# Residual products 512 columns wide by token tile, with weights kept whole, norms a tile behind, and the FFN in three parts

## The chip, the cores and the metric

The kernel runs on one core of one Trainium2 chip. The metric is the device time of one execution in microseconds (us); lower is better, and the median of several executions counts. TensorE (PE) does matrix products and transposes, VectorE (DVE) and ScalarE (ACT) work element by element, GpSimd (POOL) does a few tiny operations, and SyncE (SP) issues nearly all loads.

## The reference

Two layers over two streams of 256 tokens each: the latents (stream 0) and a context (stream 1), with 1024 features. The context is needed in layer 0 alone; layer 1 computes the latents only. Cut to what matters here:

```python
hx = modulate(rmsnorm(x, mix_pre_g[l]), shx1, scx1)          # and hc for the context
yx, yc = mixer_layer(hx, hc, ...)    # four branches, gates, their sum @ w_out
x = x + gx1 * rmsnorm(yx, mix_post_g[l])
fx = swiglu(modulate(rmsnorm(x, ffn_pre_g[l]), shx2, scx2), w_ffn1[l], w_ffn3[l], w_ffn2[l])
x = x + gx2 * rmsnorm(fx, ffn_post_g[l])
# shifts, scales and gates of a layer: silu(c) @ ada_w[l] + ada_b[l], six rows of 1024
def swiglu(h, w1, w3, w2):           # d_ff = 2816, 22 tiles of 128
    return (jax.nn.silu(h @ w1) * (h @ w3)) @ w2
```

## The kernel before

All values are float32. A product is made of three passes over parts in the type float32r: each operand is split into a high part h (one copy on ScalarE, L87) and a low part l (one subtraction on VectorE, L90), and `gemm` runs h·h, h·l and l·h (L162 to L164) for each tile of 128 along the sum. For the weights the parts are `wh` and `wl`, pairs of 128x512.

Weights are not kept on the chip. `wload` brings 512 KB at a time into one of four buffers `raw` (issued by SyncE, L126), splits it into two pairs, and calls `tick`. Each tick lets a share of background work run: the modulation vectors of a later stage, from `ada_w`. A load of 512 KB goes to a buffer `araw` (L346), which is one of the same four, and VectorE adds its columns to accumulators `acc` (L98), later turned by a STREAM_TRANSPOSE (L324) and a reduction (L325). The rate per weight pair is a constant for each stage.

The program runs, for each layer, a mixer, the product with `w_out` and a feed-forward part (FFN). By the trace: start up to 55 us, mixer 0 to 444, out 0 to about 500, FFN 0 to about 885, mixer 1 to 1134, out 1 to 1170, FFN 1 to the end. Each engine executes its instructions in a fixed order that the build decides, and it may place an instruction ahead of one that the code writes first. Pools of buffers are opened for a stage and closed after it; the memory of a stage's pool is that of the stage before it.

A residual product (`mixer` after the branches, with mT as the turned input, and the second half of `ffn`, with G) gives y, token-major, for each tile of 128 tokens: four tiles in layer 0, two in layer 1. It goes through four column blocks of 256. In each, all token tiles run together with the sum outermost, so the weights are taken as they come; ScalarE squares the result with a sum (`sq`), VectorE multiplies it by the gate row (`y`). The last block goes one token tile after the other (`last_gemm`), and each tile is normed at once: `postnorm` sums the squares (`vp`, L437), takes a reciprocal root on GpSimd (`rp`), adds to the residual stream `x`, squares that on ScalarE; `normed` takes another root (`vn`, `rn`) and scales into `y`; `turn_in` transposes it on TensorE (L171) in 8 blocks of 128, and `modulated` (after the stream's second tile) applies shift and scale (`hm`) and splits into the next stage's input h. In the FFN, G is made and used in two halves of 11 feature tiles. A residual product of the second half adds to the first half's y.

At the end of a mixer the last gate products are followed on VectorE by `th`, `m` and the split of mT (L98), and the gate rows G are made by eight L389 products.

## Time and profile before

| what | value |
| --- | --- |
| median of 3 executions | 1365.78 us (1362.2 to 1367.07) |
| span of the profiled execution | 1368.4 us |
| TensorE busy | 1309.4 us |
| VectorE busy | 998.5 us |
| ScalarE busy | 687.9 us |

The span is from the first to the last instruction of one profiled execution; no other time is listed for it. Busy times of engines overlap. TensorE's busy time includes the modelled ends of products that run into one another, so what a product costs in a row of like ones is seen from the distance of their starts.

### The profile page before, as it was taken

What the parts mean: (1) busy time and instruction counts of PE and PEld (TensorE: products, weight loads), DVE (VectorE), ACT (ScalarE), POOL (GpSimd) and SP (SyncE); (2) the same over time, 40 slices, a digit from 0 to 9 for tenths busy, and PEclk for the clock granted to TensorE, in tenths of its full rate; (3) what the DMA queues carried; (4) which work ended last, traced back from release to release, by engine and by line L of the source; (5) the groups of instructions that cost most, each with busy time, mean ns of one, the idle gap of its engine ahead of it and who ended that gap; (6) DMA issues with size and microseconds to landing.
All of it is one profiled execution on the core that took longest, in us unless ns stands there. A gap on an engine that the chain in (4) does not pass through costs nothing.

```text
span 1368.4 us, 22990 instructions
## 1 busy us (share of the span) xinstructions
PE 1309.4 (96%) x8525; PEld 1155.2 (84%) x8525; DVE 998.5 (73%) x2162; ACT 687.9 (50%) x1611; POOL 45.2 (3%) x66
## 2 busy tenths in 40 slices
PE   5998999999999989999999999888899998899997
PEld 1697777887778988889988889878799998899997
DVE  4846688777899989987457664656887887665665
ACT  2634556546555545333353333554766666555653
POOL 1021000000000010000000000100000000000000
PEclk9999999999999999999999999999999999899999
DMA  8615222223236635665556653144342435455552
GB/s 299 206 49 153 85 70 78 76 84 103 85 102 198 203 121 162 206 200 186 179 162 215 185 167 96 47 154 154 93 124 58 152 117 167 133 181 185 180 174 98
DMA packets 167940, 194.66 MB, mean 142 GB/s; under 512 B 6682, under 2 KB 141140, under 8 KB 167572
## 3 DMA queue, kind: packets, MB, share of 16 engines
q1 hardware_dynamic: 166500, 188.73, 43.7%
q0 software_dynamic: 1312, 4.46, 1.1%
q8 instruction: 67, 1.10, 0.3%
q14 instruction: 45, 0.37, 0.1%
q10 hardware_dynamic: 16, 0.00, 0.0%
HBM read 192.12 MB, written 1.05 MB: 141 GB/s over the span
## 4 chain that ended last, share of the span: by engine, by line
PE 80%; DVE 9%; DMA 4%; ACT 3%; POOL 2%; issue 2%; SPq 0%; DVEq 0%; POOLq 0%; ACTq 0%
PE g L162 23%; PE g L164 23%; PE g L163 23%; PE a L573 3%; PE a L171 3%; PE a L624 2%; DVE grp L90 1%; DVE wl L90 1%; ACT grp L87 1%; PE g L293 1%; DVE acc L98 1%; DMA ada<-in_ada_w_dram 1%; POOL rq L114 1%; DMA raw<-in_w_in_dram 1%; DVE zq L90 1%
## 5 line engine op out<-in xcount | busy, mean ns | idle before, releaser
L87 ACT ACTIVATE wh<-raw 128x512 fp32r<-128x512 f32 (+2 forms) x520 | 317.8, 620 | 354.5 <-PE g L163 136.0
L90 DVE TENSOR_TENSOR wl<-raw,wh 128x512 fp32r<-128x512 f32 (+2 forms) x520 | 346.4, 677 | 162.9 <-ACT wh L87 157.2
L162 PE MATMUL g<-h,wh 128*128 128x256 f32 (+1 forms) x1248 | 415.5, 336 | 3.6 <-DVE grp L90 1.2
L164 PE MATMUL g<-h,wl 128*128 128x256 f32 (+1 forms) x1248 | 415.2, 334 | 0.9 <-DVE wl L90 0.9
L163 PE MATMUL g<-h,wh 128*128 128x256 f32 (+1 forms) x1248 | 415.1, 334 | 0.0
L162 PEld LDWEIGHTS g<-h,wh 128*128 128x128 f32 x1248 | 235.6, 190 | 28.1 <-ACT h L87 1.8
L164 PEld LDWEIGHTS g<-h,wl 128*128 128x128 f32 x1248 | 236.7, 190 | 23.6 <-DVE wl L90 1.1
L163 PEld LDWEIGHTS g<-h,wh 128*128 128x128 f32 x1248 | 236.8, 190 | 21.7 <-DVE h L90 0.4
L98 DVE SCALAR_TENSOR_TENSOR acc<-araw,cs,acc 128x512 f32<-128x512 f32 x224 | 162.4, 749 | 78.8 <-DMA araw<-in_ada_w_dram 60.8
L164 PE MATMUL g<-wh,g 128*128 128x256 f32 x528 | 149.4, 283 | 0.0
L162 PE MATMUL g<-wh,g 128*128 128x256 f32 x528 | 149.2, 283 | 0.0
L163 PE MATMUL g<-wl,g 128*128 128x256 f32 x528 | 148.3, 281 | 0.0
L162 PE MATMUL g<-wh,h 128*128 128x256 f32 (+2 forms) x336 | 99.4, 297 | 2.2 <-DVE m L98 1.2
L163 PE MATMUL g<-wl,h 128*128 128x256 f32 (+2 forms) x336 | 99.1, 296 | 1.3 <-DVE wl L90 1.0
L163 PEld LDWEIGHTS g<-wl,g 128*128 128x128 f32 x528 | 100.0, 189 | 0.1
L162 PEld LDWEIGHTS g<-wh,g 128*128 128x128 f32 x528 | 99.4, 188 | 0.1
L164 PEld LDWEIGHTS g<-wh,g 128*128 128x128 f32 x528 | 98.9, 187 | 0.0
L164 PE MATMUL g<-wh,h 128*128 128x256 f32 (+2 forms) x336 | 98.3, 294 | 0.0
L98 DVE SCALAR_TENSOR_TENSOR th<-th,g 128x512 f32<-128x512 f32 (+1 forms) x136 | 71.3, 549 | 6.4 <-PE g L164 3.6
L162 PEld LDWEIGHTS g<-wh,h 128*128 128x128 f32 x336 | 64.2, 191 | 4.8 <-issue 1.7
L87 ACT ACTIVATE th<-g 128x512 f32<-128x512 f32 (+1 forms) x108 | 51.5, 486 | 31.3 <-PE g L164 30.3
L163 PEld LDWEIGHTS g<-wl,h 128*128 128x128 f32 x336 | 64.0, 191 | 3.4 <-DVE wl L90 2.4
(184 smaller groups left out, 1908.3 us busy)
## 6 DMA issues: line engine op xcount, KB each, us to landing
raw<-in_w_ffn_dram SPq DMA_DIRECT2D x120, 512.0 KB
raw<-in_w_in_dram SPq DMA_DIRECT2D x84, 512.0 KB
araw<-in_ada_w_dram SPq DMA_DIRECT2D x80, 512.0 KB
ada<-in_ada_w_dram SPq DMA_DIRECT2D x16, 512.0 KB
raw<-in_w_branch_dram SPq DMA_DIRECT2D x32, 256.0 KB
raw<-in_w_out_dram SPq DMA_DIRECT2D x16, 512.0 KB
raw<-in_w_ffn_dram SPq DMA_DIRECT2D x16, 384.0 KB
raw<-in_w_in_dram SPq DMA_DIRECT2D x8, 416.0 KB
```

What stands on the lines that cost most here:

```text
L87: return self.nc.scalar.activation(out, in_, func, **k)
L90: return self.nc.vector.tensor_tensor(out=out, in0=a, in1=b, op=op)
L98: return self.nc.vector.scalar_tensor_tensor(out=out, in0=a, scalar=s, in1=b, op0=op0, op1=op1)
L114: self.nc.gpsimd.tensor_tensor(out=r, in0=v, in1=self.mhalf[:, 0:n], op=ALU.pow)
L162: mm(ps, ah, bh, start=k == 0 and opens, stop=False, skip_group_check=True)
L163: mm(ps, ah, bl, start=False, stop=False, skip_group_check=True)
L164: mm(ps, al, bh, start=False, stop=last, skip_group_check=True)
L171: self.nc.tensor.transpose(out, in_, self.ident[0:k, 0:k])
L293: self.nc.tensor.matmul(ps[j][0:2], self.cs[:, :, k], raw[j, h, k], start=k == cut[j], stop=k == NK - 1)
L573: nc.tensor.matmul(ps[:, 0:nk], x, y, start=i == 0, stop=i == len(mms) - 1 and not masked)
L624: nc.tensor.matmul(po[:, 0:256], grp[:, 4, kts[k] * 128:kts[k] * 128 + 128], pt[j][:, k], start=j == 0 and k == 0, stop=j == 1 and k == n - 1)
```

## The change

`residual()` takes the place of the column blocks and of `last_gemm`. The products of a token tile are 512 columns wide, two column blocks to a tile, and go one tile after the other. So all weights of both blocks must be there for a tile to be done; for `w_out` they lie in 16 pairs of their own (tags `oh`, `ol`) in the stage's pool, for the last FFN part half of them lie in buffers of G (tag `G2`). After a tile's products comes `chain` (the norms); `turn` (transposes, shift and scale) of a tile is written behind the next tile's products, and the last tile's turn is put off: `flush` calls it in the FFN behind the first products of stream 0 (layer 0), at its beginning (layer 1), and in mixer 1 behind the first products of its branch A, which are moved ahead of the pooling branch for that. The last tile's normed result goes to a buffer of the tag `raw`. The turned features go to one fixed set of tiles, `H`, which also serves as mT. The FFN is done in three parts of 8, 8 and 6 feature tiles. The pairs wh, wl have 8 buffers each in place of 7.

```diff
-WB = 7
+WB = 8
...
+PARTS = ((0, 8), (8, 8), (16, 6))
...
+        self.late = self.qp = None
+        self.H = [tuple(self.hp.tile([128, 512], R, tag=f"h{k}{x}", name="h") for x in "hl") for k in range(NK)]
...
+    def bank(self):
+
+        self.turn8 = (self.turn8 + 1) % 8
+        return self.pg() if self.turn8 < 4 else self.pa()
...
-    def h_tiles(self, name):
-        return [tuple(self.hp.tile([128, 512], R, tag="h", name=name, bufs=16) for _ in range(2)) for _ in range(NK)]
+    def flush(self):
+
+        late, self.late = self.late, None
+        if late:
+            late()
...
-    def last_gemm(self, h, w, nk, s, evac, norm):
-        """The last product of a stream's residual, a token tile after the other, each normed at once."""
-        for t in range(2):
-            ps = self.pg()[:, 0:256]
-            self.gemm([(ps, self.cols_of(h, self.tok(s, t)), w, True)], nk)
-            evac(3, {(s, t): ps})
-            norm(t)
+    def residual(self, lhs, w, nk, tiles, evac, chain, turn):
+
+
+        for i, k in enumerate(tiles):
+            for cb in range(2):
+                ps = self.pg()
+                self.gemm([(ps, self.cols_of(lhs, self.tok(*k)), w[cb], True)], nk)
+                evac(cb, k, ps)
+            chain(k, i == len(tiles) - 1)
+            if turn and i:
+                turn(tiles[i - 1])
+        if turn:
+            self.late = lambda: turn(tiles[-1])
+
+    def wide(self):
+
+        return self.wp.tile([128, D], F, tag="raw", name="yn", bufs=RB)
...
+            if mT is not None and cb == 3:
+                for ft in range(NK):
+                    self.split(mT[ft][0][:, 0:n], mT[ft][1][:, 0:n], m[ft], scale=0.5)
...
+            za = self.z_gqa(l, "A", C_QA, hs, streams)
+            if l:
+                next(za)
+                self.flush()
             self.pool(l, streams, ots["D"])
             done.add("D")
-            run(self.z_gqa(l, "A", C_QA, hs, streams))
+            run(za)
...
-            ys = {(s, t): self.tp.tile([128, D], F, tag="y", name="y", bufs=4) for s in streams for t in range(2)}
-            ssp = {k: self.sm(4, "sspp") for k in ys}
-
-            def evac(cb, pss):
-                c = slice(cb * 256, cb * 256 + 256)
-                for k, ps in pss.items():
-                    sq = self.tp.tile([128, 256], F, tag="sq2", name="sq2", bufs=2)
-                    self.act(sq, ps, AF.Square, scale=1 / 32, accum_out=ssp[k][:, cb:cb + 1])
-                    self.tt(ys[k][:, c], ps, g1[k[0]][:, c], ALU.mult)
-
-            for cb in range(4):
-                w = self.wunit(self.d["w_out"][l], cb * 256, 256)
-                if cb < 3:
-                    evac(cb, self.tok_gemm(mT, w, 256, [streams], NK))
-            drain(self.bg)
-            ab2 = {s: self.ab(l, "ffn", s) for s in streams}
-            h2 = self.h_tiles("h2")
-            for s in streams:
-                if l == 0:
+            tiles = [(s, t) for s in streams for t in range(2)]
+            ys = {k: self.tp.tile([128, D], F, tag="y", name="y", bufs=4) for k in tiles}
+            ssp = {k: self.sm(2, "sspp") for k in tiles}
+            pss = {s: {} for s in streams}
+            if l == 0:
+                for s in streams:
                     xs[s] = self.load_x(s)
-                pss = {}
-
-                def norm(t):
-                    y, x = ys[s, t], xs[s][t]
-                    self.normed(x, self.postnorm(y, ssp[s, t], x), y)
-                    self.turn_in(t, y, pss, range(0, NK, 2))
-
-                self.last_gemm(mT, w, NK, s, evac, norm)
-                self.modulated(s, pss, ab2[s], h2)
-        return h2
+
+            def evac(cb, k, ps):
+                c = slice(cb * 512, cb * 512 + 512)
+                sq = self.tp.tile([128, 512], F, tag="sq2", name="sq2", bufs=2)
+                self.act(sq, ps, AF.Square, scale=1 / 32, accum_out=ssp[k][:, cb:cb + 1])
+                self.tt(ys[k][:, c], ps, g1[k[0]][:, c], ALU.mult)
+
+            def chain(k, last):
+                y, x = ys[k], xs[k[0]][k[1]]
+                if last:
+                    ys[k] = self.wide()
+                self.normed(x, self.postnorm(y, ssp[k], x), ys[k])
+                if k == tiles[0]:
+                    drain(self.bg)
+
+            def turn(k):
+                s, t = k
+                self.turn_in(t, ys[k], pss[s], range(0, NK, 2))
+                if t == 1:
+                    self.modulated(s, pss[s], self.ab(l, "ffn", s), self.H)
+
+            pair = lambda: tuple(self.tp.tile([128, 512], R, tag="o" + x, name="w" + x, bufs=16) for x in "hl")
+            w = [self.wunit(self.d["w_out"][l], cb * 512, 512, pair=pair) for cb in range(2)]
+            self.residual(mT, w, NK, tiles, evac, chain, turn)
+        return self.H
...
+        def up(w, ps, c):
+            self.gemm([(ps[f][:, c], fs(w, f), self.cols_of(h2, c), c.start == 0) for f in range(2)], NK)
...
+        for part, (f0, nf) in enumerate(PARTS):
             G = []
-            for fb in range(f0, f0 + half, 2):
-                nf = min(2, f0 + half - fb)
-                pss = []
+            for fb in range(f0, f0 + nf, 2):
+                units = []
                 for w in (w1, w3):
-                    wu = self.wunit(w, fb * 128, nf * 128)
-                    ps = [self.pg()[:, 0:n] for _ in range(nf)]
-                    # the first products take a stream after the other, as they come
-                    for c in [slice(s * 256, s * 256 + 256) for s in streams] if fb == 0 else [slice(0, n)]:
-                        self.gemm([(ps[f][:, c], fs(wu, f), self.cols_of(hn, c), c.start == 0) for f in range(nf)], NK)
-                    if w is w1:
-                        ths = []
-                        for f in range(nf):
-                            th = fp.tile([128, 512], F, tag="th", name="th", bufs=TB)[:, 0:n]
-                            self.act(th, ps[f], AF.Tanh, scale=0.5)
-                            self.stt(th, th, 1.0, ps[f], ALU.add, ALU.mult)
-                            ths.append(th)
-                for f in range(nf):
-                    self.stt(ths[f], ths[f], 0.5, ps[f], ALU.mult, ALU.mult)
-                    gh, gl = (fp.tile([128, 512], R, tag="G2", name="g2", bufs=FB)[:, 0:n] for _ in range(2))
-                    self.split(gh, gl, ths[f])
-                    G.append((gh, gl))
-                if g2 is None and f0:
+                    wu = self.wunit(w, fb * 128, 256)
+                    units.append((wu, [self.bank()[:, 0:n] for _ in range(2)]))
+                    if fb:
+                        up(*units[-1], slice(0, n))
+                        if w is w1:
+                            ths = silu(units[0][1])
+                if not fb:
+
+                    for s in streams:
+                        for u in units:
+                            up(*u, slice(s * 256, s * 256 + 256))
+                        self.flush()
+                    ths = silu(units[0][1])
+                for f in range(2):
+                    self.stt(ths[f], ths[f], 0.5, units[1][1][f], ALU.mult, ALU.mult)
+                    g = tuple(x[:, 0:n] for x in pair())
+                    self.split(*g, ths[f])
+                    G.append(g)
...
+            if part < len(PARTS) - 1:
+                for cb in range(2):
+                    w = self.wunit(w2, cb * 512, 512, f0, nf)
+                    pss = {k: self.bank() for k in tiles}
+                    self.gemm([(ps, self.cols_of(G, self.tok(*k)), w, True) for k, ps in pss.items()], nf)
+                    for k, ps in pss.items():
+                        evac(cb, k, ps)
         for _ in self.bg:
             pass
-        for s in streams:
-            step = after(s)
-            self.last_gemm(G, w, half, s, evac,
-                           lambda t: step(t, ys[s, t], self.postnorm(ys[s, t], ssp[s, t], xs[s][t], square)))
-            step(2, None, None)
+        w = [self.wunit(w2, cb * 512, 512, f0, nf, pair=pair if cb else None) for cb in range(2)]
+
+        def chain(k, last):
+            ss = self.postnorm(ys[k], ssp[k], xs[k[0]][k[1]], square)
+            if last and turn:
+                ys[k] = self.wide()
+            after(k, ys[k], ss)
+
+        self.residual(G, w, nf, tiles, evac, chain, turn and (lambda k: turn(k, ys[k])))
```

Three places show how the order of instructions moves. Names: `wl`, `raw`, `acc`, `araw`, `th`, `m`, `y` as above; `h_91` to `h_94` in the changed kernel are the parts of mT's last two feature tiles, `yn` is the last token tile's normed result.

On VectorE at the end of mixer 0 and the head of out 0, before:

```order
L90 TENSOR_TENSOR wl_4814<-raw_4811,wh_4813 128x512
L98 SCALAR_TENSOR_TENSOR acc_4633<-araw_4829,cs_98,acc_4633 128x512
L98 SCALAR_TENSOR_TENSOR acc_4634<-araw_4829,cs_98,acc_4634 128x512
L90 TENSOR_TENSOR wl_4820<-raw_4811,wh_4819 128x512
L98 SCALAR_TENSOR_TENSOR th_4695<-th_4695,g_4709 128x512
L98 SCALAR_TENSOR_TENSOR th_4697<-th_4697,g_4710 128x512
L90 TENSOR_TENSOR m_922<-m_922,th_4695 128x512
L90 TENSOR_TENSOR m_922<-m_922,th_4697 128x512
L90 TENSOR_TENSOR wl_4826<-raw_4823,wh_4825 128x512
L90 TENSOR_TENSOR wl_4834<-raw_4823,wh_4833 128x512
```

and in the changed kernel:

```order
L102 SCALAR_TENSOR_TENSOR acc_4605<-araw_4837,cs_114,acc_4605 128x512
L102 SCALAR_TENSOR_TENSOR th_4667<-th_4667,g_4681 128x512
L102 SCALAR_TENSOR_TENSOR th_4669<-th_4669,g_4682 128x512
L94 TENSOR_TENSOR m_922<-m_922,th_4667 128x512
L94 TENSOR_TENSOR m_922<-m_922,th_4669 128x512
L102 SCALAR_TENSOR_TENSOR acc_4606<-araw_4837,cs_114,acc_4606 128x512
L102 SCALAR_TENSOR_TENSOR h_92<-m_922,h_91 128x512
L102 SCALAR_TENSOR_TENSOR h_94<-m_922,h_93 128x512
L102 SCALAR_TENSOR_TENSOR acc_4605<-araw_4837,cs_114,acc_4605 128x512
L102 SCALAR_TENSOR_TENSOR acc_4606<-araw_4837,cs_114,acc_4606 128x512
L336 STREAM_TRANSPOSE araw_4837<-acc_4605 128x512
L94 TENSOR_TENSOR wl_4806<-raw_4803,wh_4805 128x512
```

The first four splits of w_out stood ahead of, and right behind, the last `th` and `m`; the first one (`wl_4806`) now stands behind these, behind both splits of mT, behind four `acc` rows of one load (`araw_4837`) and behind a transpose of the accumulator.

On TensorE at the end of out 0, before, from the transposes of the context's first tile:

```order
L171 MATMUL a_5486<-ident_82,y_4805 128x128 x2
L171 MATMUL a_5489<-ident_82,y_4805 128x128 x2
L164 MATMUL g_5632<-h2_5284,wl_5610 128x256
L162 MATMUL g_5631<-h2_5286,wh_5617 128x256
L171 MATMUL a_5492<-ident_82,y_4805 128x128 x2
L163 MATMUL g_5631<-h2_5287,wh_5617 128x256
L164 MATMUL g_5631<-h2_5286,wl_5618 128x256
L162 MATMUL g_5632<-h2_5286,wh_5617 128x256
```

and in the changed kernel, from the last residual product:

```order
L171 MATMUL g_5235<-wh_4927,h_94 128x512
L178 MATMUL a_5280<-ident_98,y_4789 128x128 x2
L178 MATMUL a_5283<-ident_98,y_4789 128x128 x2
L178 MATMUL a_5286<-ident_98,y_4789 128x128 x2
L178 MATMUL a_5289<-ident_98,y_4789 128x128 x2
L178 MATMUL a_5280<-ident_98,yn_5263 128x128 x2
L178 MATMUL a_5283<-ident_98,yn_5263 128x128 x2
L178 MATMUL a_5286<-ident_98,yn_5263 128x128 x2
L178 MATMUL a_5289<-ident_98,yn_5263 128x128 x2
L169 MATMUL g_5341<-h_79,wh_5306 128x256
```

Where FFN products (`h2` with `wh`) stood between the transposes of the context's tiles, those of its last two tiles now stand together, and the first FFN product (`g_5341`) comes behind them. VectorE there, in the changed kernel, from the last tile's residual sum:

```order
L102 SCALAR_TENSOR_TENSOR x_4801<-y_4790,rp_5267,x_4801 128x512 x2
L99 TENSOR_SCALAR vn_5274<-ssn_5269 128x1
L98 TENSOR_SCALAR yn_5263<-x_4801,rn_5276 128x512 x2
L99 TENSOR_SCALAR hm_5490<-a_5280,adac_4603,adac_3990 128x256
L94 TENSOR_TENSOR h_80<-hm_5486,h_79 128x256
L99 TENSOR_SCALAR hm_5498<-a_5283,adac_4603,adac_3990 128x256
L94 TENSOR_TENSOR h_82<-hm_5490,h_81 128x256
L94 TENSOR_TENSOR h_84<-hm_5494,h_83 128x256
L94 TENSOR_TENSOR wl_5307<-raw_5304,wh_5306 128x512
L94 TENSOR_TENSOR wl_5320<-raw_5304,wh_5319 128x512
```

The first split of the FFN's weights, `wl_5307`, now stands behind `yn` and behind five steps of the turned features.

On TensorE at the end of out 1 in the changed kernel, from the last residual product:

```order
L171 MATMUL g_12146<-wh_12042,h_94 128x512
L178 MATMUL a_12191<-ident_98,y_11962 128x128 x2
L178 MATMUL a_12194<-ident_98,y_11962 128x128 x2
L178 MATMUL a_12197<-ident_98,y_11962 128x128 x2
L178 MATMUL a_12200<-ident_98,y_11962 128x128 x2
L178 MATMUL a_12191<-ident_98,yn_12174 128x128 x2
L178 MATMUL a_12194<-ident_98,yn_12174 128x128 x2
L178 MATMUL a_12197<-ident_98,yn_12174 128x128 x2
L178 MATMUL a_12200<-ident_98,yn_12174 128x128 x2
L169 MATMUL a_12272<-h_79,wh_12254 128x256
```

Here too, all transposes of both tiles stand together, ahead of the first FFN product. At the end of FFN 0 it is the same: 8 transposes of `yn` stand between the last residual product and the first product of mixer 1; 96 products of the pooling branch's input and of branch A then stand ahead of the first product that reads `band`, a load into mixer 1's pool.

The numbers of products change as follows: those of 256 columns from 5498 to 3338, those of 512 from 2080 to 3160.

## Rows read from the trace of the kernel before

**Rows 1.** The page: span, busy time of each engine.

```profile
span 1368.4 us, 22990 instructions
...
PE 1309.4 (96%) x8525; PEld 1155.2 (84%) x8525; DVE 998.5 (73%) x2162; ACT 687.9 (50%) x1611; POOL 45.2 (3%) x66
```

**Rows 2.** Stretches: length; busy PE, PEld, DVE, ACT, POOL; PEclk, DMA share, GB/s.

```profile
444.00:490.00 46.00, 46.00 (x381) 45.37 (x380) 41.18 (x77) 21.57 (x56) 1.54 (x2) 1.00 0.63 204
490.00:516.00 26.00, 20.71 (x152) 19.09 (x152) 23.68 (x56) 15.58 (x42) 5.52 (x7) 0.93 0.22 74
516.00:600.00 84.00, 84.00 (x428) 70.89 (x428) 80.29 (x139) 35.89 (x66) 0.00 (x0) 1.00 0.60 192
858.00:908.00 50.00, 41.30 (x318) 38.08 (x318) 35.43 (x85) 28.09 (x78) 5.96 (x9) 0.97 0.32 103
1130.00:1180.00 50.00, 42.71 (x330) 41.57 (x330) 35.69 (x75) 31.15 (x75) 2.19 (x4) 0.90 0.43 137
1361.00:1368.40 7.40, 0.36 (x4) 0.16 (x2) 2.82 (x7) 0.51 (x2) 0.55 (x1) 0.79 0.38 142
```

**Rows 3.** Timeline of PE (start, duration): 512 columns, 10 starts apart.

```profile
435.12 0.39 PE L164 MATMUL g<-h,wl 128*128 128x512 f32 x1
...
437.39 0.39 PE L162 MATMUL g<-h,wh 128*128 128x512 f32 x1
```

**Rows 4.** Timeline of PE: 256 columns at the head of out 0, 11 starts apart.

```profile
446.14 0.28 PE L162 MATMUL g<-wh,mT 128*128 128x256 f32 x1
...
447.46 0.28 PE L164 MATMUL g<-wh,mT 128*128 128x256 f32 x1
```

**Rows 5.** Groups of PE by form: residual products, one of three alike.

```profile
L162 PE MATMUL g<-wh,g 128*128 128x256 f32 x528 | 149.2, 283 | 0.0
...
L162 PE MATMUL g<-wh,mT 128*128 128x256 f32 x192 | 55.0, 286 | 0.0
```

**Rows 6.** Timeline of DVE around the head of out 0.

```profile
443.86 1.37 DVE L98 SCALAR_TENSOR_TENSOR th<-th,g 128x512 f32<-128x512 f32 x2
...
446.36 1.28 DVE L90 TENSOR_TENSOR wl<-raw,wh 128x512 fp32r<-128x512 f32 x2
...
447.56 0.68 DVE L98 SCALAR_TENSOR_TENSOR mT<-m,mT 128x512 fp32r<-128x512 f32 x1
...
449.41 1.41 DVE L98 SCALAR_TENSOR_TENSOR acc<-araw,cs,acc 128x512 f32<-128x512 f32 x2
...
452.66 1.30 DVE L324 STREAM_TRANSPOSE araw<-acc 128x512 f32<-128x512 f32 x2
```

**Rows 7.** Timelines of SP and ACT: a w_out load, its first use.

```profile
451.48 0.37 SPq L126 DMA_DIRECT2D raw<-in_w_out_dram  x1
...
455.73 0.63 ACT L87 ACTIVATE wh<-raw 128x512 fp32r<-128x512 f32 x1 [0.98 <-DMA raw<-in_w_out_dram]
```

**Rows 8.** Timeline of PE at the end of out 0.

```profile
490.56 0.28 PE L163 MATMUL g<-wl,mT 128*128 128x256 f32 x1
...
493.52 1.06 PE L171 MATMUL a<-ident,y 128*128 128x128 f32 x8 [2.68 <-DVE y L94]
```

**Rows 9.** Waits of PE from 858 to 908 us.

```profile
PE a L781 <- DMA band<-in_pool_dram: 4.0, 1, 4.0
```

**Rows 10.** Timelines of PE and DVE at the end of out 1.

```profile
1157.95 0.28 PE L164 MATMUL g<-wh,mT 128*128 128x256 f32 x1
...
1160.62 0.42 DVE L90 TENSOR_TENSOR y<-g,G 128x256 f32<-128x256 f32 x1
...
1167.46 1.97 PE L171 MATMUL a<-ident,y 128*128 128x128 f32 x8 [3.45 <-DVE y L94]
...
1169.26 1.22 PE L162 MATMUL g<-h,wh 128*128 128x256 f32 x4
...
1170.70 0.28 PE L163 MATMUL g<-h,wh 128*128 128x256 f32 x1
```

More of the change, by code (lines that the diff above doesn't have):

```diff
@@ L129, in wload @@
             m = min(step, nk - k0)
[L130 removed]
+            h, l = (pair or self.wpair)()
             self.split(h[:, 0:m * n], l[:, 0:m * n], rv[:, k0:k0 + m].rearrange("p k n -> p (k n)"))
@@ L955, in ffn, with silu @@
-        for f0 in (0, half):
+        pair = lambda: tuple(fp.tile([128, 512], R, tag="G2", name="g2", bufs=FB) for _ in range(2))
+        if len(streams) == 1:
+            self.flush()
+        def up(w, ps, c):
+            self.gemm([(ps[f][:, c], fs(w, f), self.cols_of(h2, c), c.start == 0) for f in range(2)], NK)
+        def silu(ps):
+            ths = []
+            for f in range(2):
+                th = fp.tile([128, 512], F, tag="th", name="th", bufs=TB)[:, 0:n]
+                self.act(th, ps[f], AF.Tanh, scale=0.5)
+                self.stt(th, th, 1.0, ps[f], ALU.add, ALU.mult)
+                ths.append(th)
+            return ths
@@ new lines, in ffn, with evac @@
+                if g2 is None and part:
+                    g2 = self.gate_rows(l, "ffn", streams)
+            def evac(cb, k, ps):
+                c = slice(cb * 512, cb * 512 + 512)
+                y = ys[k][:, c]
+                if part == 0:
+                    self.act(y, ps)
+                    return
+                self.tt(y, ps, y, ALU.add)
+                if part == len(PARTS) - 1:
+                    sq = fp.tile([128, 512], F, tag="sq2", name="sq2", bufs=2)
+                    self.act(sq, y, AF.Square, scale=1 / 32, accum_out=ssp[k][:, cb:cb + 1])
+                    self.tt(y, y, g2[k[0]][:, c], ALU.mult)
@@ L1041, in run, with after, turn @@
         h2 = self.mixer(0, xs, h1, both)
-        h1 = []
-        def to_next(s):
-            if not h1:
-                h1.extend(self.h_tiles("h1"))
-            pss = {}
-            def step(t, y, ss):
-                if t < 2:
-                    self.normed(xs[s][t], ss, y)
-                    self.turn_in(t, y, pss, range(0, NK, 2))
-                else:
-                    self.modulated(s, pss, self.ab(1, "mix", s), h1)
-            return step
+        pss = {s: {} for s in both}
+        def after(k, y, ss):
+            self.normed(xs[k[0]][k[1]], ss, y)
+        def turn(k, y):
+            s, t = k
+            self.turn_in(t, y, pss[s], range(0, NK, 2))
+            if t == 1:
+                self.modulated(s, pss[s], self.ab(1, "mix", s), self.H)
         def steps():
```

63 lines of the change are left out of this document (26 added, 37 removed).

## The prediction

> **What bounds the kernel now.** I read the page first. TensorE is busy for 1309.4 of 1368.4 us, VectorE for 998.5 [rows 1]: products set the time, and a change helps by making them cheaper or by closing TensorE's gaps. So I then read the busy times by stretch [rows 2]. The reader is to see there that TensorE has no gap in the first 46 us of out 0 and in the first 84 us of FFN 0, and that the gaps lie where one stage hands over to the next: 5.3 us idle in 490 to 516 (out 0 to FFN 0), 8.7 in 858 to 908 (FFN 0 to mixer 1), 7.3 in 1130 to 1180 (out 1 to FFN 1), and 7 at the end. The granted clock in these stretches is 0.90 to 0.97, so some products behind the gaps ran at the lower level of 1.2 GHz. In both gapless stretches VectorE is nearly as busy as TensorE: 41.2 of 46 and 80.3 of 84 us. A change that puts VectorE's work ahead of what TensorE needs there has little slack. Last I read the timelines of single instructions, for the costs below.
>
> The median of the three runs is 1365.78 us; the profiled execution's span is 2.6 us (0.2%) above it. I make the sum against the span and take 2.6 off at the end. The three runs lie within 0.36% of one another; 0.5% (6.8 us) is about what a measurement of this kernel can tell from no change.
>
> **Width of the products.** Ten starts of 512 columns lie 2.27 us apart, 0.227 each [rows 3]; eleven of 256 columns 1.32, 0.120 each [rows 4]. Two of the narrow ones, 0.240, become one wide one: 13 ns saved. The residual products are 3 x (528 + 192) = 2160 [rows 5] and become 1080, as the counts in the section on the change say. 1080 x 13 ns = **-14.0 us**. The rows are read to 0.01 us, so 13 to 15; 0 if wide residual products should cost what two narrow ones do, which no row suggests, since the wide products of [rows 3] have the same tile of 128x128 as their fixed operand.
>
> The Trainium skill, page "TensorE: Matmul & The Clock Gate", section "Back-to-back issue gap", gives the spacing of isolated products as columns / 2.4 plus 2.5 ns: 109 ns for 256 and 216 for 512. By that a merged pair would save 2.5 ns and the change 2.7 us, an estimate, and the sum would be 11 us higher than mine. The trace does not agree, 120 and 227 ns; here the part that doesn't grow with the columns is about 13 ns. The measurement decides.
>
> **Head of out 0.** Before, the first splits of w_out are made ahead of the mixer's last `th`, and TensorE goes on without a gap [rows 2]. After, the order on VectorE is: an `acc` row that needs the load araw_4837, two `th`, two `m`, an `acc`, two splits of mT, two `acc`, a transpose, and only then the first split, for w_out's pairs now lie in the memory that the mixer's pool held. `th` began at 443.86 and with `m` took 2.5 us until the split at 446.36; an `acc` is 0.67 to 0.7, a split or mT step 0.6, a transpose 0.65 [rows 6]. From `th` to the first split: 2.5 + 3 x 0.67 + 2 x 0.6 + 0.6 = 6.3 us. `th` itself starts late if the load does: one took 4.2 us from its issue to its first use [rows 7]. Between no delay and 4.2 us I take 2.6, because the load is asked for a few rows earlier: `th` at 446.5, the first split at 452.8 (450.2 to 454.4), where the first product stood at 446.14 [rows 4].
>
> From there to the last split VectorE has 16 splits, 12 `acc`, 3 transposes, 4 reductions and a `y`: 9.6 + 8.0 + 1.8 + 2.4 + 0.6 = 22.4 us, so 475.2. The loads say about the same: 12 of 512 KB at the 204 GB/s of that stretch [rows 2] take 31 us from 444. With waits for one another I take 477 (475 to 482). Products of the first two token tiles fill this time, 96 x 0.227 = 21.8 us. They would be done at 446.1 + 21.8 = 467.9, and are done at about 478: **+10 us** (+7 to +14). The first tile's transposes then stand 27 products (6.1 us) behind, and its norms take about 6.5 (below), so **+1** (0 to 2).
>
> **Handovers.** The change puts the last tile's turn off, but in the order shown its transposes stand directly behind the last residual product and ahead of the first FFN product, and the split of the first FFN weights stands behind `yn`. So the last tile's norms lie open on TensorE. Their length from out 1 of before [rows 10]: `y` at 1160.62 to the transposes at 1167.46 is 6.8 us, with a scaling of the other tile and weight splits in between; alone I take 5.0. Ahead of it come the end of the product (0.4), a square of 512 columns (about 0.6, as wide as the copy in [rows 7]) and a `y` twice as wide: 6.5 us from the last product to the transposes (5.5 to 8.5). From the transposes to products at their full spacing were 3.2 us (1167.46 to 1170.70). Of these 9.7 us TensorE fills some 2.8 with 16 transposes at 0.13 (eight took 1.06 in [rows 8]) and six products. About 7 are lost, and I add 2 for the lower clock behind the gap and the late first weights: 9 (6 to 11) for each handover.
>
> Out 0: before, 5.3 idle, 1.8 of clock (0.07 x 26) and about 1 that modelled ends hide, since a product is shown as 0.28 long and stands 0.12 from the next; one such gap is that from 490.56 to 493.52 [rows 8]. 9 - 8 = **+1**. FFN 0: before, 8.7 + 1.5 + 1 = 11; of it 4.0 is a wait for `band` [rows 9], which 96 products (11.5 us) now stand ahead of, but the last tile's norms take its place. 10 - 11 = **-1**. Out 1: before, 1157.95 to 1170.70 [rows 10], 12.75 less 2.8 of work, 10. After, a head that was not there (6 steps of 256 columns at 0.42 as `y` in [rows 10] and a split of 0.6, so 3.1, with no `acc` among them) and a tail of 9.5: **+2.6**. At the end of the kernel a square and two VectorE steps are twice as wide, 0.42 against 0.69: **+0.7**.
>
> Three FFN parts add a set of sums to y on VectorE and take away some splits of half-filled pairs; TensorE's number of tiles stays. This is hidden by FFN 0's and FFN 1's products where VectorE has room; where it has none is the second rival. The copying of mT to `H` and the moved splits cost nothing as long as the first k's are ready when the first product is, which waits for weights anyway.
>
> **Sum.** -14.0 + 10 + 1 + 1 - 1 + 2.6 + 0.7 = +0.3: a span of 1368.7, on the median's scale **1366 us**. The width pays, and the new places of the splits and of the last norms take it back.
>
> **The rivals.**
> 1. *The stalls are shorter than worked out* (faster). Nothing else runs on VectorE and ScalarE beside the last tile's norms, which speaks for 6 instead of 9 to 10 at three handovers: -10, 1356 us. Or the head of out 0 loses 3 instead of 10, if the load for `acc` is there in time and the splits come before their products need them: 1359. Against it: the chain's length is the rows' own. If the turn were truly hidden behind the next stage, tails of 2 us would give -22, 1344; the order speaks against it.
> 2. *VectorE becomes the bound of FFN 0's start* (slower). With 80.3 of 84 us it has 3.7 to spare [rows 2]. It decides once what out 0 leaves behind (late `acc` work, wider `y`) is more than that; at 10% over, 8 us, and the time is 1374. Or the 12 loads of out 0, which share four buffers, come slower than 204 GB/s: at two thirds of it the last split stands at 490 and not 477, +13, 1379.
> 3. *The wide products save nothing* (slower): +14, 1380. Only the skill's figure speaks for something near it.
>
> **How the numbers follow.** My forecast 0.45 (its own range 1360 to 1372), shorter stalls 0.26, hidden turn 0.05, VectorE or loads as the bound 0.20, no gain by width 0.04. Faster takes rival 1 but for cases at its edge, slower takes rivals 2 and 3, and a little of the forecast's spread goes to either side: 0.30 faster, 0.44 same, 0.26 slower. Leaving out the hidden turn, the slowest loads and rival 3 gives 1351 to 1378.
>
> **What would show it.** Starts of wide residual products 0.227 apart; in out 0 a gap of 6 to 7 us ahead of the first one, its end by VectorE's split, and the first two tiles paced by splits for some 22 us; at the three handovers a TensorE gap of 5 to 7 us that `yn` ends, with a granted clock near 0.5 behind it; no wait for `band`. Wrong would be: no such gap in out 0, gaps at the handovers that other products fill, or a VectorE busy share of 100% with TensorE gaps between weight splits in FFN 0.

## The result and the profile after

The changed kernel takes 1400.57 us in the median (1398.58 to 1403.0, 4 runs), the kernel before 1366.42 beside it: a ratio of 1.0243 (95% interval 1.021 to 1.0277), 34 us slower. The profiled execution spans 1401.2 us, 32.8 more than that of before [rows 1].

The page of the changed kernel, span and busy times, answers to [rows 1]:

```profile
span 1401.2 us, 20596 instructions
PE 1317.4 (94%) x7445; PEld 1108.5 (79%) x7445; DVE 1002.3 (72%) x2130; ACT 680.1 (49%) x1543; POOL 43.3 (3%) x66
```

VectorE's work is the same; TensorE has 1080 products fewer and still a longer busy time, at a granted clock of 0.976 in the mean where the kernel before had 0.990. Busy time by stretch (columns as in [rows 2]), changed kernel:

```profile
57.00:67.00 10.00, 7.59 (x64) 7.38 (x62) 4.88 (x9) 4.28 (x11) 0.59 (x1) 1.00 0.88 287
122.00:138.00 16.00, 9.32 (x35) 6.77 (x34) 11.88 (x23) 10.87 (x36) 3.07 (x4) 0.81 0.32 98
456.00:470.00 14.00, 8.29 (x25) 5.88 (x24) 12.42 (x20) 6.59 (x13) 0.53 (x1) 0.76 0.44 143
516.00:530.00 14.00, 7.36 (x37) 6.22 (x36) 7.99 (x19) 6.96 (x17) 1.10 (x2) 0.81 0.12 37
684.00:696.00 12.00, 6.74 (x23) 5.11 (x22) 7.92 (x14) 5.42 (x11) 0.00 (x0) 0.83 0.43 130
905.00:925.00 20.00, 10.41 (x52) 8.70 (x51) 15.22 (x34) 12.51 (x31) 2.12 (x4) 0.74 0.34 106
1191.00:1203.00 12.00, 5.23 (x28) 4.42 (x26) 7.02 (x17) 6.35 (x17) 1.10 (x2) 0.75 0.14 41
```

Four of these are handovers that the prediction spoke of (out 0's head and end, FFN 0's end, out 1's end). Three are not: two places in mixer 0, and the FFN's gate rows at 684; around those of the kernel before, from 700 to 730 us, its TensorE waits for nothing. In six of the seven the granted clock is 0.74 to 0.83 in the mean: part of the products behind a gap ran at the lower of its two levels, 1.2 GHz. What TensorE waited for in the whole execution (total in us, times, longest):

```profile
PE a L178 <- DVE yn L98: 17.2, 3, 6.7
PE g L169 <- ACT wh L91: 12.8, 6, 5.2
...
PE a L169 <- ACT G L91: 5.3, 1, 5.3
PE g L169 <- DVE m L102: 4.8, 3, 3.9
...
PE a L811 <- DMA band<-in_pool_dram: 3.1, 1, 3.1
```

`yn` is the last token tile's norms at the three handovers, 5.2 to 6.7 us each, as predicted. `wh` is w_out's first splits and the first weights of the next stage. `G` is the unpredicted stall in FFN 0.

To compare the stages I worked out a lost time for each from the starts of TensorE's products: the length of the stage less the sum of its products at 0.2267 us (512 columns), 0.120 (256) or 0.109 (128). It holds gaps, the lower clock and spacings above these; products of other widths are the same in all these kernels. The stages end at marks that stand in both kernels: gate rows of out 0 and out 1, last transposes of out 0, FFN 0 and out 1, last product.

| lost, us | to out 0 | out 0 | FFN 0 | mixer 1 | out 1 | FFN 1 |
| --- | --- | --- | --- | --- | --- | --- |
| before | 59.5 | 7.8 | 10.0 | 28.8 | 9.3 | 1.1 |
| changed | 71.7 | 20.5 | 26.1 | 26.1 | 12.3 | 6.1 |
| h2_turn_at_once | 66.9 | 19.6 | 23.7 | 29.2 | 11.0 | 4.8 |
| e1_own | 76.6 | 18.4 | 22.8 | 32.2 | 14.0 | 5.1 |
| e2_noload | 82.0 | 17.9 | 18.8 | 27.1 | 11.6 | 5.0 |
| e3_narrow | 70.4 | 17.8 | 15.4 | 27.6 | 11.0 | 3.6 |
| e4_pg | 64.8 | 20.3 | 27.3 | 27.9 | 13.1 | 6.1 |
| f1_wb7 | 68.0 | 17.7 | 18.9 | 27.5 | 11.7 | 5.4 |
| f2_hm | 61.1 | 19.5 | 18.5 | 27.7 | 12.6 | 5.9 |
| f3_oldout | 71.6 | 8.9 | 18.0 | 27.3 | 9.3 | 3.7 |
| f4_prefetch | 72.0 | 14.1 | 23.5 | 26.6 | 11.7 | 2.9 |
| h1_head | 68.3 | 19.0 | 20.7 | 27.2 | 8.1 | 5.3 |
| g1_ffn_only | 59.6 | 7.1 | 15.8 | 27.8 | 9.3 | 4.1 |
| g2_ffn_narrow | 59.4 | 7.6 | 13.4 | 31.7 | 9.3 | 1.6 |
| g3_before_wide | 61.9 | 6.3 | 19.9 | 24.1 | 9.4 | 2.5 |
| g4_prefetch_all | 60.8 | 13.6 | 25.7 | 26.2 | 12.1 | 4.1 |

Each row is one profiled execution, and that can lie some us off its run's median (e1's 7 above, f2's and g2's 4 above, e3's and h2's 4 below), so rows are compared stage by stage. The changed kernel and the runs e3, e4, f3, f4, h1 and h2 have the same order of instructions up to out 0, on VectorE and ScalarE but for a few rows at its end, and lose 64.8 to 72.0 us there, so a single row of that column is good to some 4 us. From before to changed the losses grow by 12.2 + 12.7 + 16.1 - 2.7 + 3.0 + 5.0 = 46.3 us, the end behind the last product by 1.0, and the products' sum at these spacings falls by 14.4: 32.9, where the spans differ by 32.8.

The width: residual products of 512 columns in FFN 0, start and duration, nine starts apart, to be read against [rows 3, 4]:

```profile
639.61 0.40 PE L169 MATMUL g<-wh,g 128*128 128x512 f32 x1
...
641.71 0.40 PE L169 MATMUL a<-wh,g 128*128 128x512 f32 x1
```

2.10 us for nine, 0.2333 each, where the wide products of [rows 3] stand 0.227 apart. A merged pair saves 6.7 ns, not 13.

The head of out 0, VectorE and then TensorE, with the idle time before an instruction and what ended it in brackets:

```profile
457.54 0.75 DVE L102 SCALAR_TENSOR_TENSOR acc<-araw,cs,acc 128x512 f32<-128x512 f32 x1 [3.53 <-DMA araw<-in_ada_w_dram]
458.21 1.27 DVE L102 SCALAR_TENSOR_TENSOR th<-th,g 128x512 f32<-128x512 f32 x2
...
464.43 3.66 DVE L94 TENSOR_TENSOR wl<-raw,wh 128x512 fp32r<-128x512 f32 x6
```

TensorE in the same stretch, its first product with w_out:

```profile
463.87 0.80 PE L169 MATMUL g<-wh,h 128*128 128x512 f32 x1 [5.24 <-ACT wh L91]
```

This is the prediction's head of out 0: `th` waits behind an `acc` whose load is late, and VectorE's first split comes 6.2 us after `th`. What ends TensorE's gap is ScalarE's part of the first split, `wh`, and not VectorE's. The same pattern, an `acc` row that waits and `th` behind it, stands where the prediction did not look, at FFN 0's gate rows. The timeline of the changed kernel there, SyncE's issue, VectorE and TensorE:

```profile
685.69 0.37 SPq L358 DMA_DIRECT2D araw<-in_ada_w_dram  x1
...
690.35 0.75 DVE L102 SCALAR_TENSOR_TENSOR acc<-araw,cs,acc 128x512 f32<-128x512 f32 x1 [4.08 <-DMA araw<-in_ada_w_dram]
691.02 1.28 DVE L102 SCALAR_TENSOR_TENSOR th<-th,g 128x512 f32<-128x512 f32 x2
...
692.90 0.79 PE L169 MATMUL a<-h,wh 128*128 128x512 f32 x1 [5.26 <-ACT G L91]
```

The load is issued at 685.69 and used at 690.35; `th` comes only behind it, ScalarE's copy of `th` behind that, then ScalarE's `G` that empties a bank, and TensorE wants this bank. It idles 5.3 us and then starts at half its rate (0.79 long against 0.39).

### The profile page after: what moved, and what is told of

The parts are those of the page before. It is cut to its first block, busy times and chain, and to the rows that moved or that the text cites. A ratio compares the mean times of both kernels' runs of the same rounds, so it can differ in the third digit from the quotient of the medians.

```text
span 1401.2 us, 20596 instructions
## 1 busy us (share of the span) xinstructions
PE 1317.4 (94%) x7445; PEld 1108.5 (79%) x7445; DVE 1002.3 (72%) x2130; ACT 680.1 (49%) x1543; POOL 43.3 (3%) x66
## 4 chain that ended last, share of the span: by engine, by line
PE 81%; DVE 8%; ACT 4%; DMA 3%; issue 1%; POOL 1%; SPq 0%; POOLq 0%; DVEq 0%; ACTq 0%
PE g L169 18%; PE g L170 17%; PE g L171 17%; PE a L169 6%; PE a L170 6%; PE a L171 6%; PE a L603 3%; PE a L178 3%; PE a L654 2%; PE g L305 2%; DVE wl L94 2%; DMA araw<-in_ada_w_dram 1%; ACT grp L91 1%; DVE grp L94 1%; DVE acc L102 1%
## 5 line engine op out<-in xcount | busy, mean ns | idle before, releaser
L91 ACT ACTIVATE wh<-raw 128x512 fp32r<-128x512 f32 (+1 forms) x500 | 304.5, 626 | 341.0 <-PE g L170 101.7
L94 DVE TENSOR_TENSOR wl<-raw,wh 128x512 fp32r<-128x512 f32 (+1 forms) x500 | 333.6, 684 | 141.9 <-ACT wh L91 138.3
L169 PE MATMUL g<-h,wh 128*128 128x256 f32 (+1 forms) x896 | 302.6, 339 | 4.2 <-ACT wh L91 1.5
L170 PE MATMUL g<-h,wh 128*128 128x256 f32 (+1 forms) x896 | 300.2, 336 | 0.0
L171 PE MATMUL g<-h,wl 128*128 128x256 f32 (+1 forms) x896 | 299.1, 336 | 0.0
L169 PEld LDWEIGHTS g<-h,wh 128*128 128x128 f32 x896 | 171.1, 191 | 23.0 <-ACT wh L91 1.9
L170 PEld LDWEIGHTS g<-h,wh 128*128 128x128 f32 x896 | 171.2, 191 | 15.6 <-issue 0.2
L169 PE MATMUL g<-wh,h 128*128 128x256 f32 (+3 forms) x432 | 139.7, 326 | 12.8 <-ACT wh L91 11.3
L170 PE MATMUL g<-wl,h 128*128 128x256 f32 (+3 forms) x432 | 139.4, 324 | 0.8 <-DVE wl L94 0.7
L171 PE MATMUL g<-wh,h 128*128 128x256 f32 (+3 forms) x432 | 138.3, 321 | 0.0
L169 PE MATMUL a<-h,wh 128*128 128x256 f32 (+1 forms) x352 | 119.3, 339 | 6.7 <-ACT G L91 5.3
L170 PE MATMUL a<-h,wh 128*128 128x256 f32 (+1 forms) x352 | 118.7, 337 | 0.0
L171 PE MATMUL a<-h,wl 128*128 128x256 f32 (+1 forms) x352 | 117.8, 337 | 0.0
L169 PEld LDWEIGHTS a<-h,wh 128*128 128x128 f32 x352 | 68.9, 196 | 14.1 <-ACT G L91 5.7
L170 PEld LDWEIGHTS a<-h,wh 128*128 128x128 f32 x352 | 68.9, 196 | 6.5
L171 PEld LDWEIGHTS a<-h,wl 128*128 128x128 f32 x352 | 68.3, 195 | 6.5
```

Source lines behind the costliest of these rows:

```text
L91: return self.nc.scalar.activation(out, in_, func, **k)
L94: return self.nc.vector.tensor_tensor(out=out, in0=a, in1=b, op=op)
L169: mm(ps, ah, bh, start=k == 0 and opens, stop=False, skip_group_check=True)
L170: mm(ps, ah, bl, start=False, stop=False, skip_group_check=True)
L171: mm(ps, al, bh, start=False, stop=last, skip_group_check=True)
```

## The experiments

Theory A, from those two places and two more in mixer 0 (an `acc` waits 2.7 us at 127 and 2.2 at 242): the loss comes from `acc` rows that wait for loads, which get no buffer because prefetched weights hold three of the four. Theory B: it comes from the open norms at three handovers and the products' spacing.

**e1_own**: own buffers for the background's loads.

```diff
-RB = 4
-WB = 8
+RB = 3
+AB = 2
+WB = 7
-raw = self.wp.tile([128, 1024], F, tag="raw", name="araw", bufs=RB)
+raw = self.wp.tile([128, 1024], F, tag="araw", name="araw", bufs=AB)
```

> The changed kernel, but the background loads of ada_w have two buffers of their own and the weights three (raw), in place of four shared; wh and wl have 7 buffers each. Theory A (VectorE's queue is held by acc rows that wait for a load which gets no buffer, because prefetched weights hold them: at 127, 242, 457 and 690 us of the changed kernel's trace): the gaps behind these waits shrink, together 10 to 16 us, so about 1386 to 1390 us. Theory B (the loss is the last tiles' norms at three handovers and the products at 233 ns, and the acc waits only lie beside them): within 4 us of 1400.

**e2_noload**: the background reads one tile, loaded once; a second one takes its transposes. Like e1, it also has seven weight buffers in place of eight.

```diff
-WB = 8
+WB = 7
...
-raw = self.wp.tile([128, 1024], F, tag="raw", name="araw", bufs=RB)
-self.nc.sync.dma_start(raw.rearrange("p (k n) -> p k n", k=2), w[:, k:k + 2, c])
+raw = self.araw[0]
```

> The changed kernel without the loads of ada_w after the first: every acc row reads one resident tile, so the rows stay on VectorE and only their loads and buffers are left out (the modulation vectors are therefore not the reference's). Theory A: no acc row waits for a load, the gaps at 127, 242, 457 and 690 us go, 12 to 20 us, about 1382 to 1388 us. Theory B: within 5 us of 1400, since VectorE's work is the same.

Measured: 1402.11 us (ratio 1.0251, 1.021 to 1.0292) and 1401.96 (1.0243, 1.0217 to 1.0268). As an account of the whole loss theory A falls. By stage e2 loses 18.8 in FFN 0 instead of 26.1, and the stall at the gate rows is not there, but mixer 0 loses 82.0. The gain in FFN 0 can't be put down to the loads: f1 below, with seven buffers and all loads, loses 18.9 there, also without the stall. Both edits start with the first weights, and the order on TensorE differs from the changed kernel's from mixer 0 on, with new stalls there (in e2 one of 4.6 us behind `zr`, up to 131). So these two runs do not isolate what they were made for.

**e3_narrow**: each wide residual product as two halves of a bank.

```diff
-self.gemm([(ps, self.cols_of(lhs, self.tok(*k)), w[cb], True)], nk)
+self.gemm(self.halves(ps, self.cols_of(lhs, self.tok(*k)), w[cb]), nk)
```

> The changed kernel with each residual product of 512 columns made as two of 256 into the two halves of the same bank; all else stays. If a wide product saves 13 ns as predicted, this costs 14 us: about 1414. If it saves what the changed kernel's steady rows show (700 ns for three wide against 6 x 120 = 720 or a little more), 7 to 8 us: about 1408. No gain by width: 1400.

Measured: 1404.92 us, ratio 1.0277 (1.0245 to 1.0308), 0.34% or 4.7 us above the changed kernel's ratio: nearest to the spacings of the changed kernel's rows, but the intervals of the two overlap. g2_ffn_narrow below measures it better.

**e4_pg**: the FFN's first products in the banks g alone.

```diff
-units.append((wu, [self.bank()[:, 0:n] for _ in range(2)]))
+units.append((wu, [self.pg()[:, 0:n] for _ in range(2)]))
```

> The changed kernel with the FFN's first products in the four PSUM banks g alone, as before, in place of alternating between g and a. Theory: TensorE's gap of 5.4 us behind the FFN's gate rows at 687 us comes from a bank that the next FFN product shares with the gate rows and ScalarE empties late; without the sharing the gap goes and the time falls by 5 to 7 us, 1394. Rival: the wait moves to the next bank, since ScalarE waits for VectorE's th behind an acc row; within 2 us of 1400.

Measured: 1399.96 us, ratio 1.0234 (1.0207 to 1.0261). The time is the rival's, and FFN 0 loses 27.3, no less. But each of the two is half right. The gap at the gate rows is gone, as the theory says: from 670 to 700 us TensorE waits for nothing. Two other waits take its place, 2.4 us at 613 and 3.1 at 752, ahead of products with w_ffn2. TensorE's waits for `th` in FFN 0:

```profile
PE g L169 <- DVE th L102: 5.5, 2, 3.1
```

VectorE at the second of them:

```profile
752.94 0.75 DVE L102 SCALAR_TENSOR_TENSOR acc<-araw,cs,acc 128x512 f32<-128x512 f32 x1 [3.12 <-DMA araw<-in_ada_w_dram]
...
754.87 1.28 DVE L102 SCALAR_TENSOR_TENSOR th<-th,g 128x512 f32<-128x512 f32 x2
```

So the stall needs both, a `th` that is late and a bank that depends on it; other banks move it to another place.

Theory C then: the changed kernel's side edits reorder stages that they don't touch. Rival D: the `hm` tiles hold up mixer 0's load of `band`. The section on the change does not tell of them: they came from a pool that lasts through the kernel, and the change takes them from the stage's pool. The issue of `band` on GpSimd's timeline in the kernel before:

```profile
51.32 0.59 POOL L763 DMA_DIRECT2D band<-in_pool_dram  x1 [18.39 <-PE a L171]
```

and in the changed kernel:

```profile
59.23 0.59 POOL L793 DMA_DIRECT2D band<-in_pool_dram  x1 [25.57 <-DVE h L94]
```

It waited for a transpose before, and waits for VectorE's last split of the first h now, since `hm` lies where the mixer's pool comes.

**f1_wb7** (`WB = 8` to `WB = 7`, nothing else).

> The changed kernel with 7 buffers each for wh and wl in place of 8; all else stays. Theory C (the 12 us that mixer 0 loses come from its order of instructions, which is another one with 8 buffers; with 7 it is nearly the order of before): mixer 0 ends 8 to 12 us earlier, 1390 to 1393 us. Rival D (they come from the load of band, which waits for the hm tiles that now lie in the stage's pool, and what follows that wait): at most 2 us, 1399, with the wait for band still there. Theory A has fallen with the runs before: no load at all left the time where it was.

**f2_hm** (`WB = 7`, and `hm` always from the lasting pool, as before).

```diff
-if self.tp is self.qp:
-    return self.qp.tile([128, 512], F, tag="th", name="hm", bufs=TB)[:, 0:256]
-return self.tp.tile([128, 256], F, tag="hm", name="hm", bufs=HB)
+return self.ap_.tile([128, 256], F, tag="hm", name="hm", bufs=HB)
```

> The changed kernel with 7 buffers each for wh and wl and the hm tiles back in a pool that lasts through the kernel, as before. Theory C: mixer 0 as in the run with 7 buffers alone, and 3 us more from the wait for band: 1386 to 1390. Rival D: 4 to 6 us by the wait for band and its following, 1395, and the run with 7 buffers alone at 1399.

Measured: 1386.6 us, ratio 1.0126 (1.0094 to 1.0159), and 1381.18, 1.0095 (1.0064 to 1.0126). The seven buffers give 14 to 16 us, more than the 8 to 12 of theory C, and not where it said: mixer 0 loses 68.0, inside what the runs with eight lose there. FFN 0 gains 7.2, out 0 2.8. VectorE at FFN 0's gate rows with seven buffers:

```profile
679.54 1.38 DVE L102 SCALAR_TENSOR_TENSOR th<-th,g 128x512 f32<-128x512 f32 x2 [0.91 <-PE g L171]
...
683.25 0.75 DVE L102 SCALAR_TENSOR_TENSOR acc<-araw,cs,acc 128x512 f32<-128x512 f32 x1 [1.14 <-DMA araw<-in_ada_w_dram]
```

Here `th` stands ahead of the `acc` row that waits, and TensorE does not wait at this place. Mixer 0 is rival D's: with seven buffers alone `band` is issued at 58.70 and TensorE waits 3.2 us for it, and with `hm` in the lasting pool it is issued at 52.24, there is no wait for it, and mixer 0 loses 61.1 against 59.5 before; the three other runs with that edit lose 59.4 to 60.8. The step from f1 to f2 is 5.4 us in the medians, where D said 4 to 6; D's total for f1, 1399, was far off. With eight buffers `hm` was not moved back by itself. GpSimd's timeline of f2_hm:

```profile
52.24 0.60 POOL L791 DMA_DIRECT2D band<-in_pool_dram  x1 [19.11 <-PE g L170]
```

**f3_oldout**: the w_out product of before (column blocks of 256, `last_gemm`) in the changed kernel.

> The changed kernel with the w_out product of before in both layers (four column blocks of 256 as the weights come, the last one by token tile with its norms and turn at once); FFN parts and mixers as changed. Theory (the head and the open norms of out 0 and out 1 cost 14 us beside what they gain by width): out 0 by 12 and out 1 by 3 us shorter, the time 1385 to 1388. Rival (the stalls follow from what mixer and FFN leave to VectorE, whatever the products' order): within 3 us of 1400.

**f4_prefetch**: the FFN's first weights asked for ahead of the residual products.

```diff
+self.first_f = [self.wunit(self.d[f][l], 0, 256) for f in ("w_ffn1", "w_ffn3")]
 self.residual(mT, w, NK, tiles, evac, chain, turn)
...
-wu = self.wunit(w, fb * 128, 256)
+wu = self.wunit(w, fb * 128, 256) if fb else self.first_f[w is w3]
```

> The changed kernel, but the FFN's first two weight units are asked for ahead of the residual products of out 0 and out 1, so their loads and splits come before the last tile's norms, and 96 FFN products of stream 0 stand ahead of the last tile's transposes in out 0. Theory (TensorE waits 5.3 us for the last tile's norms and 1.8 for the first FFN weights, with the lower clock behind them, for want of these products): out 0 to FFN 0 loses 6 to 9 us less, out 1 1 to 2, so 1390 to 1394. Rival (the earlier splits take VectorE and ScalarE from w_out's and the gain is given back): 1398 to 1403.

Measured: 1381.24 us, ratio 1.0086 (1.0056 to 1.0116), and 1389.89, 1.015 (1.0121 to 1.0178). Both theories hold in their stages: with the old w_out out 0 loses 8.9 and out 1 9.3, as before the change (7.8 and 9.3); with the prefetch out 0 loses 14.1 instead of 20.5, and FFN 1 2.9 instead of 6.1. TensorE's waits over the whole execution with the prefetch:

```profile
PE a L178 <- DVE yn L98: 12.0, 2, 6.7
```

Two waits for `yn` in place of three: at the end of out 0 the put-off turn is now behind products and costs nothing. At out 1 there is one stream, so its products need the last tile. Of f3's gain another 8 us is in FFN 0, where the gate rows' stall was smaller (3.0 us), without an edit there.

**h1_head**: w_out's first four pairs in `wh` and `wl` buffers.

```diff
-w = [self.wunit(self.d["w_out"][l], cb * 512, 512, pair=pair) for cb in range(2)]
+own = lambda n=[0]: (n.__setitem__(0, n[0] + 1), self.wpair() if n[0] <= 4 else pair())[1]
+w = [self.wunit(self.d["w_out"][l], cb * 512, 512, pair=own) for cb in range(2)]
```

> The changed kernel with the first four of w_out's 16 pairs in wh and wl buffers, which are free there, and the other twelve in the stage's pool as changed. Theory (the first split waits for memory that the mixer's pool still holds, as the prediction said of the head of out 0): these splits stand ahead of the mixer's last steps, TensorE's gap of 5.4 us ahead of the first residual product shrinks to 0 to 2, out 0 takes 4 to 7 us less, 1394 to 1397. Rival (VectorE's pace over the 16 splits and the acc rows sets the first two tiles anyway): the gap moves behind the fourth pair and the time stays within 2 us of 1400.

**h2_turn_at_once**: `self.late = lambda: turn(tiles[-1])` becomes `turn(tiles[-1])`.

> The changed kernel with the last tile's turn called at once in place of being put off into the next stage. Theory (in the changed kernel's order the put-off turn stands ahead of the next stage's products anyway, since these wait for weights): within 3 us of 1400. Rival (the turn was put behind some products after all): 4 us or more longer.

Measured: 1390.33 us, ratio 1.0162 (1.0135 to 1.0189), and 1400.52, 1.0248 (1.022 to 1.0275). At the head the first product no longer waits, but in out 0 the rival is right; TensorE's waits there between 450 and 470 us:

```profile
PE g L170 <- DVE wl L94: 3.5, 3, 2.4
PE g L169 <- ACT wh L91: 1.8, 1, 1.8
```

5.3 us of waits for later splits in place of one gap of 5.2, and out 0 loses 19.0 against 20.5. Of the 11 us gained, 4.2 are in out 1, where no `acc` rows stand among the splits, and 5.4 in FFN 0, again without an edit there. Putting the turn off or not makes no difference, as the changed order led to expect.

Four runs put pieces together.

> The FFN of the changed kernel with the rest as before: w_out in four column blocks of 256, 7 buffers each for wh and wl, the hm tiles in the pool that lasts. If the three repairs add up (20 us by the hm tiles and 7 buffers, 20 by w_out, of which out 0's start may count in both): 1360 to 1365, a ratio of 0.994 to 0.998. If they repair the same stalls twice: 1372 to 1380.

> The kernel of the run before with each residual product of the FFN made as two of 256 columns; the order of the rest stays close. 792 wide products at stake: 10.5 us longer if a wide one saves 13 ns, 5 to 6 if it takes 233 ns against 2 x 120, 0 if width is worth nothing.

> The kernel before with its first two column blocks of every residual product made one of 512 columns, as the weights come; the last two and the order of norms stay. 540 wide products: 7 us shorter at 13 ns each, 4 us at 7 to 8 ns, so a ratio of 0.995 to 0.997; 1.000 if the wider evacuations hold the banks up as long.

> The changed kernel with 7 buffers, the hm tiles in the pool that lasts and the FFN's first two weight units asked for ahead of the residual products: all that the change meant to do, with its side effects repaired. Additive: 1381 less 8 to 12, 1368 to 1373, a ratio of 0.999 to 1.003; the head of out 0 (6 us) and the norms at the two other handovers stay open. Not additive: 1378.

- **g1_ffn_only** (f3 and f2 together): 1365.78 us against 1368.94 before, ratio 0.9978 (0.9965 to 0.999). The repairs add up, and this is the one version that is shorter than the kernel before, by 0.2%. Its waits for the last tiles, four with the old form in out 0 and out 1 and one in the changed form at FFN 0's end:

```profile
PE a L178 <- DVE y L98: 11.5, 4, 3.8
...
PE a L178 <- DVE yn L98: 6.6, 1, 6.6
```

- **g2_ffn_narrow** (g1 with the edit of e3): 1373.96 us, 1.0031 (1.0019 to 1.0043), 8.2 longer; in its profile the two FFNs are 5.9 us longer, 7.4 ns for each of 792 products, and 3.9 lie in mixer 1, which the edit doesn't touch. So a wide product is worth about 7 ns.
- **g3_before_wide** (the kernel before with `BLK = (slice(0, 512), slice(512, 768), slice(768, 1024))` as column blocks): 1371.28 us, 1.0022 (1.0005 to 1.0039), a miss. TensorE's work falls by 3.6 us (540 x 6.7 ns), and FFN 0 loses 9.9 more, over half of it in one wait of TensorE for the end of a background step on VectorE:

```profile
PE a L332 <- DVE vsum L326: 5.6, 1, 5.6
```

- **g4_prefetch_all** (f2 and f4 together): 1382.74 us, 1.0101 (1.0085 to 1.0116), no better than f2 alone. Out 0 loses 13.6 instead of 19.5, and FFN 0 25.7 instead of 18.5, in several new waits, the longest 2.8 us for a `th`.

## Why the prediction was wrong

It forecast 1366 us (1351 to 1378) and no change; the kernel takes 1400.57, 34 us more, above the range and above every rival's time. Against the sum of +0.3:

- **Width, -14.0.** The step failed in its size. It took the spacing of one kind of wide product, `h` past weights in [rows 3], for that of all. The residual ones stand 0.2333 apart, and g2 gives 7.4 ns for each: about -7. "No row suggests" a smaller saving is not so: in the kernel before, the wide products `g<-o,wh` are 401 to 411 ns long in the groups by form, `g<-h,wh` 392 to 393, and stand 0.234 apart (rows in the last section). The Trainium skill's 2.5 ns for isolated products (page "TensorE: Matmul & The Clock Gate", section "Back-to-back issue gap") are too few by these rows; the measured 7 lie between them and the forecast's 13.
- **Head of out 0, +11, and its handover, +1.** Right: the late load, `th`, the splits and their pace are there as worked out, the first product 7.3 us behind the gate rows' start, and out 0 loses 12.7 more, 1.3 of it by the spacing. f3 shows that the w_out product in its new form is the cause. h1 corrects the reading: the late first split sets nothing by itself, the pace of the splits among `acc` rows does.
- **Handovers.** Right in kind: the last norms lie open at all three, 5.2 to 6.7 us with the lower clock behind them, and h2 shows that putting the turn off changes nothing in this order. The stage out 1 came out as worked out (+3.0 for +2.6 and 0.6 of spacing), but 2.0 of its tail, a wait of 1.5 for the FFN's first weights and a slow start, stand in FFN 1's column. At FFN 0 the prediction had -1 (with 10 us for what it gives as 9 elsewhere, without a reason); by the products' starts this handover lost 11.2 before and 11.1 after: the wait for `band` went, as it said, but the last norms take 6.7 and the first weights of mixer 1 another 2.0. The end is +1.0 for +0.7.
- **What was costed at nothing.** This is the step that failed most. The eighth buffer and the move of `hm` into the stage's pool have no term in the sum, and so mixer 0 and the inside of FFN 0 have none; the prediction says only that the three FFN parts are "hidden by FFN 0's and FFN 1's products where VectorE has room". The parts nearly are: g1, which keeps them, loses 2.3 us in FFN 0 and 1.3 in FFN 1 beyond the wider spacing. What was missed is the order elsewhere. Mixer 0 lost 12 us in the profile (5 to 12 over the runs with that order), among them 3.1 of waiting for `band`, which the prediction looked for at mixer 1 alone; `hm` in its old pool gives 7 of it back in the profiles of f1 and f2, 5.4 in the medians. FFN 0 lost 8.2 at its gate rows by the products' starts, 5.4 as a gap and 2.8 in slow products behind it, where an `acc` row now stands ahead of `th`. This comes and goes with edits elsewhere: seven buffers alone take it away.
- **The rival.** "VectorE becomes the bound of FFN 0's start" was not how it went; at the gate rows VectorE was busy for 7.92 of 12 us and idle for 4.1 behind one row that waited for a load. No rival had that, and none came above 1380.

From 0.3 to 32.8, then: width 7, mixer 0 12, FFN 0 with the handover behind it 11 (8.2 at the gate rows, 1.5 behind the last transposes of out 0, 1 for the handover), FFN 1 3. In the table FFN 0's column shows more, because the handover's waits now lie ahead of the last transposes; the 2.7 less in mixer 1 is the other side of that. What mixer 0 lost beside `hm` has no cause shown. Why a few instructions change places when a buffer count changes is not shown by any run here; that they do, and that it costs 8 us at one place, is.

## What to carry to other kernels

In a kernel whose engines run fixed orders, an edit to buffers or pools can change the order anywhere: list the instructions that may only start when memory comes free (here one load, `band`, behind `hm`), and look in the new order for rows that wait on a load ahead of rows that TensorE needs. A put-off step is put off only if the work to hide it is ready: ask for its weights first, as f4 did (out 0 lost 6 less; but g4 shows that this gain did not add to f2's). When an experiment's total stays where it was, compare stage by stage: e2 gained 7 us in FFN 0 and lost 10 in mixer 0. And when an edit carries a second one along, as e1 and e2 also took the eighth weight buffer away, run the second one alone before crediting the first: f1 gained the same 7.

## What was not expected of the hardware

Wide products of one shape have two spacings: 0.227 us in [rows 3] and 0.2333 for the residual ones. It is not that weights stream past tokens in the one and tokens past weights in the other. In the kernel before, the products with w_branch have the tokens `o` streaming past a tile of weights, as [rows 3] have `h`, and stand 2.57 us apart over eleven starts, 0.234 each:

```profile
427.37 0.40 PE L162 MATMUL g<-o,wh 128*128 128x512 f32 x1
...
429.94 0.40 PE L164 MATMUL g<-o,wl 128*128 128x512 f32 x1
```

The last products of the changed kernel, with their weights in buffers of G, stand 0.226 apart (1391.72 to 1392.85, five starts), but over all 107 distances of that kind the mean is 0.229. What makes the difference is open; no run took it apart. And one order of instructions takes mixer 0 through with 64.8 to 72.0 us lost from one execution to another, while the totals of the changed kernel's four executions lie within 4.4 us.
